# Gates kept raw until the merge, a scan-ordered S5 state, and S5 begun inside the attention, in a hybrid decoder block

## The chip, the cores and the metric

The kernel runs on one core of a Trainium2 chip. The metric is the device time of the program in microseconds (us): 1381.73 us is the median of three runs of the kernel before (1381.71 to 1381.80). The engines are named as the profile names them: PE is TensorE's matmul, PEld its weight load, DVE is VectorE, ACT is ScalarE, POOL is GpSimd, SP is SyncE, whose queue issues the DMAs here.

## The reference

One decoder block over 1024 tokens of width 1024, in float32. Two branches share one normed input: sliding-window attention (8 query heads, 2 key/value heads, blocks of 128 tokens, window 128, learned sinks and a bias by distance) and an S5 state space model (512 channels in 32 groups of 16, 64 complex states each). Sigmoid gates merge them, and a squared-ReLU MLP follows.

```
h = rmsnorm(x);  q, k, v, u, gate_a, gate_s = split(h @ w_in)
attn  = attention(q, k, v, sinks, bias) @ w_attn_branch
s     = gelu(s5_scan(u) + d_skip * u)          # tanh form
s     = s * sigmoid(s @ w_glu)
mixed = sigmoid(gate_a) * attn + sigmoid(gate_s) * (s @ w_ssm_branch)
y     = x + rmsnorm(mixed @ w_out);   out = y + rmsnorm(relu(h2 @ w1)^2 @ w2)
```

## The kernel before

Every float32 product is three products of rounded halves: a value is split into hi (ACT copies it rounded, L154 for weights, L161 for activations) and lo (the remainder, by DVE in L156 and L162), and mm3 (L172 to L174) adds hi·hi, hi·lo and lo·hi into one PSUM bank of 512 columns. The kernel has eight banks. Program order is the order on each engine: nothing is reordered, so an instruction that waits holds up everything written after it for the same engine. All loads and stores go through SP's queue, weights included, which arrive in pieces of 128x1024 (raw) and are split by L154 and L156 one piece ahead of their use.

The stages in order, and what the change touches in them:

- **qkv** projects the queries, the S5 input u, the keys and the values. u_evac stores u to DRAM (ud) with the token index split as k·8+j, so that a row of S5 input holds the 128 chunks k of eight tokens. L366 makes the lo parts of the keys on DVE. v_evac (L371) transposes the values on PE.
- **attention** has 16 halves (a block of 128 tokens and one key/value head) in 20 software-pipelined steps. A step puts on PE the scores of half i (L521, L522), the product with the values of half i-3 (L568) and the transposes of half i-2 (L554), then one or two pieces of filler: twelve projection matmuls each, for the gates (L1036) and, from the last steps, for stage 1. DVE adds the bias and takes the maximum (L525), ACT does Exp (L538), POOL divides (L544), ACT and DVE split the transposed probabilities. In each step from i=2, `tick(8)` feeds a side generator: ssm_tables, which computes the powers of the S5 state matrix and the tables of S5 on DVE in many small instructions (L42 in the trace, where all recorded operations have one line), runs four groups of small matmuls on PE (kernel_part, L807), adds the skip weight (L815) and stores the tables to DRAM (qd and kd). Whatever is left of them is drained behind the last step.
- **stage 1** multiplies the attention's output with its branch weights: per output tile 24 projection matmuls for the gate, a Sigmoid (L973), 12 matmuls of the branch, a product on DVE (L986) and a store (md). After each 12 matmuls `tick(11)` feeds the **ssm** generator: load1 reads u and the input weights (L850, L853), inputs() makes 8 groups of small matmuls (L869) that ACT copies into the state F, load2(0) reads the tables of the first half of the channels (L857, L861), scan() runs 18 complex multiply-adds (macc, L880 to L884, five DVE instructions) over the 128 chunks, stack() swaps halves, and outputs() runs 16 small matmul pairs per bank (L917, L918) and the tanh GELU (L921 to L927), then stores z to DRAM (zd). outputs(1) and its tables load2(1) come behind outputs(0).
- **gates 6 and 7 and glu**: z is read back (L997), split, multiplied with the glu weights (mm3), its sigmoid taken (L1019, L1020), and split again into zz. **stage 2** reads the gates (sd) and the attention branch (md) back, multiplies zz with its branch weights, multiplies by the gate (L1068), adds (L1069, POOL) and splits. The output projection and the MLP follow and are untouched.

A sequential index over 1024 tokens is split in three levels for the scan: eight tokens i in a chunk, and 128 chunks k = a·8+b. macc walks b inside each a, then carries over a.

Of the kernel before, what the change touches and what calls it, by code (L numbers as in the profile page):

```python
# [8 lines left out]
F32 = mybir.dt.float32  # L9
# [3 lines left out]
AF = mybir.ActivationFunctionType  # L13
# [4 lines left out]
P = 128  # L18
# [88 lines left out]
class Block:  # L107
# [276 lines left out]
    def u_evac(self, ps, g, h):  # L384

        nc = self.nc
        if g % 2 == 0 and h == 0:
            self.ut[g // 2] = self.r([2, 8, P])
        ut = self.ut[g // 2][:, g % 2]
        nc.scalar.activation(out=ut[:, :, 64 * h:64 * h + 64], in_=ps.rearrange("p (k j) -> p j k", j=8), func=AF.Copy)  # L390
        if h:
            nc.sync.dma_start(out=self.ud[g * P:g * P + P], in_=ut)

    def qkv(self):
        nc = self.nc
# [28 lines left out]
        for qt in range(4):  # L424
            h = qt // 2
# [47 lines left out]
        sc = self.r([2, G, 256])  # L473
        self.PT = [self.q([2, 512], F32R) for _ in range(2)]
        self.scores = [sc[:, 0], sc[:, 1], self.q([G, 256])]
        piece = self.wq.get()
        for h in range(2):
            ps = self.proj(piece, h)
            if h:
                self.wq.done()  # L480
                self.wq.pump()
            self.k_evac(ps, h)
        piece = self.wq.get()
        vt = []
        for h in range(2):
            vt.append(self.t([512]))
            ps = self.proj(piece, h)
            if h:
                self.wq.done()
                self.wq.pump()  # L490
            self.nc.scalar.activation(out=vt[h], in_=ps, func=AF.Copy)
# [84 lines left out]
    def attention(self, filler):  # L576

        late = {}

        def go(key):  # L580
            if key in late:
                next(late[key], None)

        halves = [(n, kv) for n in range(8) for kv in range(2)]
        st = {}
        for i in range(len(halves) + 4):
            if i < 16:
                n, kv = halves[i]
                if kv == 0:
                    st[n] = {"mx": self.small(NH, "mx")}  # L590
                self.a_scores(n, kv, st[n])
            go("old sm")
            if 3 <= i < 19:
                n, kv = halves[i - 3]
                late["pv"] = self.a_pv(n, kv, st[n])
                next(late["pv"])
            if 2 <= i < 18:
                n, kv = halves[i - 2]
                self.a_trans(n, kv, st[n])
            go("old pv")  # L600
            go("pv")
            late["old pv"] = late.pop("pv", iter(()))
            if i < 16:
                n, kv = halves[i]
                late["sm"] = self.a_softmax(n, kv, st[n])
                next(late["sm"])
            late["old sm"] = late.pop("sm", iter(()))
            for _ in range(1 + (4 <= i < 17) if i < 19 else 0):
                next(filler, None)
            if i >= 2:  # L610
                self.tick(8)
            if i == 0:
                self.v_evac(self.v_late, 1)

# [225 lines left out]
    def ssm(self):  # L840


        nc = self.nc
# [9 lines left out]
                nc.sync.dma_start(out=xT[hf][(7 - j) * 16:(8 - j) * 16], in_=udv[j])  # L853

        def load2(hf):
            T[hf], Q[hf] = self.r([16, P]), self.r([16, P])
            nc.sync.dma_start(out=Q[hf], in_=self.qd[hf].rearrange("c s q a t -> (c s) (q a) t"))  # L857
            kd = self.kd[256 * hf:256 * hf + 256]
            for r in range(8):
                src = bass.AP(kd.tensor, kd.offset + 16 * r, [[240, 16], [16 * 240, 16], [1, P]])  # L860
                nc.sync.dma_start(out=T[hf][r * 16:(r + 1) * 16], in_=src)  # L861

        def inputs(hf):
            for ri in range(2):
                for qb in range(2):
                    ps = self.ps().rearrange("p (q k) -> p q k", q=4)
                    for q in range(4):
                        for a in range(2):
                            nc.tensor.matmul(ps[a * DH:a * DH + DH, q, :], lhsT=W1[hf][:, ri, qb * 4 + q, a * DH:a * DH + DH],  # L869
                                             rhs=xT[hf][:, 2 * (qb * 4 + q) + a, :], start=True, stop=True)  # L870
                    q0 = 8 * hf + 4 * qb
                    nc.scalar.activation(out=F[:, ri, q0:q0 + 4, 1:P], in_=ps[:, :, 0:P - 1], func=AF.Copy)
                    yield "wait"

        def macc(dst, src, i, n):
# [8 lines left out]
            v.tensor_tensor(out=dst, in0=dst, in1=t1, op=ALU.add)  # L884

        def scan():
            Fv = F.rearrange("p c q (a b) -> p c q a b", b=8)
            for b in range(1, 8):
                macc(Fv[:, :, :, :, b], Fv[:, :, :, :, b - 1], 0, 16)
                yield 14  # L890
            for j, i in ((1, 7), (2, 8), (4, 9), (8, 10)):
                macc(Fv[:, :, :, j:16, 7], Fv[:, :, :, 0:16 - j, 7], i, 16 - j)
                yield 14
            for b in range(7):
                macc(Fv[:, :, :, 1:16, b], Fv[:, :, :, 0:15, 7], b, 15)
                yield 14

        def stack(hf):
# [9 lines left out]
        def outputs(hf):  # L908
            for gb in range(4):

                if gb % 2 == 0:
                    zt = self.q([8, P])
                ps = self.ps()
                for gi in range(4):
                    gg = gb // 2 * 8 + gb % 2 + 2 * gi
                    o = ps[:, gi * P:(gi + 1) * P]
                    nc.tensor.matmul(o, lhsT=T[hf][:, gg, :], rhs=xT[hf][:, gg, :], start=True, stop=False)  # L917
                    nc.tensor.matmul(o, lhsT=Q[hf][:, gg, :], rhs=F[:, gg % 2, 8 * hf + gg // 2, :], start=False, stop=True)  # L918

                y2, w = self.t([512]), self.t([512])  # L920
                nc.scalar.activation(out=y2, in_=ps, func=AF.Square)  # L921
                v.tensor_scalar(out=y2, in0=y2, scalar1=0.044715, scalar2=1.0, op0=ALU.mult, op1=ALU.add)
                v.tensor_tensor(out=w, in0=y2, in1=ps, op=ALU.mult)
                yield "wait"
                nc.scalar.activation(out=w, in_=w, func=AF.Tanh, scale=GELU_C)
                g4 = lambda a: a.rearrange("p (g k) -> p g k", g=4)
                v.scalar_tensor_tensor(out=zt[:, gb % 2:8:2, :], in0=g4(w), scalar=1.0, in1=g4(ps), op0=ALU.add, op1=ALU.mult)  # L927
                yield "wait"
                if gb % 2:
                    r0 = 256 * hf + gb // 2 * P  # L930
                    zv = self.zd[r0:r0 + P].rearrange("(g d) i k -> i d g k", d=16)
                    for i in range(8):
                        nc.sync.dma_start(out=zv[i], in_=zt[i * 16:(i + 1) * 16])
# [9 lines left out]
            yield from inputs(hf)  # L943
        tmp = self.q([2, 512])
        load2(0)
        yield from scan()
        yield from stack(0)
        yield from stack(1)
        yield "wait"
        yield from outputs(0)  # L950
        load2(1)
        for _ in range(5):
            yield "wait"
        yield from outputs(1)


    def stage1(self):
# [32 lines left out]
    def glu(self):  # L990
# [14 lines left out]
        for mp in range(2):  # L1005
            wh, wl = self.wq.get()
            for mi in range(2):
                m = mp * 2 + mi
                cs = slice(mi * P, mi * P + P)
                for h in range(2):  # L1010
                    ks = slice(64 * h, 64 * h + 64)
                    part = lambda z: z.rearrange("p (i k) -> p i k", i=8)[:, :, ks]
                    ps = self.ps()
                    self.mm3(ps, [((wh[:, k, cs], wl[:, k, cs]), (part(zh[k // 2][:, k % 2]), part(zl[k // 2][:, k % 2]))) for k in range(4)])
                    if (mi, h) == (1, 1):
                        self.wq.done()
                        self.wq.pump()
                    sg = self.t([8, 64])
                    nc.scalar.activation(out=sg, in_=ps.rearrange("p (i k) -> p i k", i=8), func=AF.Sigmoid, scale=0.5)  # L1019
                    nc.vector.scalar_tensor_tensor(out=sg, in0=part(zf[mp][:, mi]), scalar=0.5, in1=sg, op0=ALU.mult, op1=ALU.mult)  # L1020
                    hi, lo = (self.zz[h][:, c, m].rearrange("p (k i) -> p i k", i=8) for c in range(2))
                    self.split(sg, hi, lo)


    def gates(self, ds):
        nc = self.nc
        for d in ds:
            piece = self.wq.get()
            for h in range(2):
# [3 lines left out]
                    self.wq.done()  # L1033
                    self.wq.pump()
                sg = self.t([512])
                nc.scalar.activation(out=sg, in_=ps, func=AF.Sigmoid)  # L1036
                nc.sync.dma_start(out=self.sd[d * P:(d + 1) * P, 512 * h:512 * h + 512], in_=sg)


    def stage2(self):  # L1040
# [13 lines left out]
        for h in range(2):  # L1054
            hi, lo = self.big([8, 512]), self.big([8, 512])
            self.mT.append((hi, lo))
            sig, zz = sigs[h], self.zz[h]
            mas = ma[h]
            for dp in range(4):
                sb = self.wq.get()  # L1060
# [243 lines left out]
    def run(self):  # L1304
        with self.tc.manual_schedule():
# [1 line left out]
            self.qkv()  # L1307
            self.sd = self.dram.tile([D, L], F32, name="sd")
            s1 = self.stage1()
            self.side = [self.ssm_tables()]  # L1310
            self.attention(itertools.chain(self.gates(range(6)), s1))
            self.drain()
            self.side = [self.ssm()]
            for _ in s1:
                self.tick(11)
            self.drain()
            glu = self.glu()
            next(glu)
# [87 lines left out]
```

## Time and profile before

| | us |
|---|---|
| median of three runs | 1381.73 |
| the profiled execution's own time | 1382.77 |
| its span, first to last instruction | 1380.6 |
| mean granted clock of TensorE | 0.974 |
| PE busy | 1300.3 (94%) |
| DVE busy | 775.5 (56%) |
| ACT busy | 470.7 (34%) |
| POOL busy | 120.7 (9%) |

The span divides at the following times: queries, u, keys and values until 135.2, attention and the drained tables until 304.2, stage 1 with S5's inputs and scan until 436.4, S5's outputs and the first gate matmuls until 477.3, gates 6 and 7 until 499.1, glu until 525.7, stage 2 until 573. What comes after, 807 us, is the output projection and the MLP.

How to read it: PE is busy 94% of the span, but its busy time has a clock in it. The granted clock is a share of full speed, and the same 512 columns take 0.23 us or 0.42 us from start to start by the level of that clock. So a stretch is read three ways: how long it lasts, how much of it PE had work, and at which clock.

### The profile page before, as it was taken

To read this page: it belongs to the slowest core of one execution; us is meant where nothing else is said; L and a number is where in the kernel's file an instruction comes from. 1 tells how busy PE (TensorE), PEld (TensorE's weight loads), DVE (VectorE), ACT (ScalarE), POOL (GpSimd) and SP (SyncE) were. 2 spreads that over 40 slices of the span, in tenths; PEclk is the share of its full clock that TensorE was granted. 3 is DMA by queue.
4 is the path that set the end of the run, shared out by engine and by line. 5 is a ranking of instruction groups with operands and counts; after the bars stand their busy time and mean duration, and the time that the engine had idled before them with its cause. 6 is when DMAs were issued, how large, how long until landed. Compare 5 with 4: busy or idle time off the path is not lost.

```text
span 1380.6 us, 15685 instructions
## 1 busy us (share of the span) xinstructions
PE 1300.3 (94%) x6144; PEld 1074.8 (78%) x6144; DVE 775.5 (56%) x1367; ACT 470.7 (34%) x797; POOL 120.7 (9%) x79
## 2 busy tenths in 40 slices
PE   8999998879988499998999999999999999999997
PEld 7988876657767487876878888888888888888886
DVE  5773766661799246647862544455444554445556
ACT  4434787742112144345543112211122111221132
POOL 1000212100000003333300000000000000000014
PEclk9999999989989699999999999999999999999999
DMA  8313111248622658445611112111111111111142
GB/s 335 136 64 107 47 38 63 72 108 178 115 69 74 93 154 319 153 155 186 238 47 42 50 31 62 46 47 60 32 61 47 46 51 42 61 47 46 40 182 98
DMA packets 55065, 132.61 MB, mean 96 GB/s; under 512 B 5072, under 2 KB 22224, under 8 KB 53712
## 3 DMA queue, kind: packets, MB, share of 16 engines
q1 hardware_dynamic: 54992, 131.62, 31.2%
q8 instruction: 48, 0.79, 0.2%
q14 instruction: 25, 0.20, 0.0%
HBM read 105.94 MB, written 25.66 MB: 95 GB/s over the span
## 4 chain that ended last, share of the span: by engine, by line
PE 59%; DVE 4%; ACT 2%; DMA 1%; issue 1%; SPq 0%; DVEq 0%; ACTq 0%
PE ps L173 18%; PE ps L174 18%; PE ps L172 18%; PE ps L1152 1%; PE ps L1153 1%; PE ps L1151 1%; DVE lo L156 1%; DMA r<-kd 1%; ACT t L247 1%; DVE r L1090 1%; DMA r<-qd 0%; DVE b L162 0%; ACT b L161 0%; ACT r L1108 0%; PE ps L917 0%
## 5 line engine op out<-in xcount | busy, mean ns | idle before, releaser
L172 PE MATMUL ps<-b,hi 128*128 128x512 f32 x976 | 387.3, 397 | 7.7 <-DVE t L815 5.4
L174 PE MATMUL ps<-b,lo 128*128 128x512 f32 x976 | 383.6, 393 | 7.8 <-DVE lo L156 7.8
L173 PE MATMUL ps<-b,hi 128*128 128x512 f32 x976 | 383.3, 393 | 0.9 <-DVE b L162 0.9
L154 ACT ACTIVATE hi<-raw 128x1024 fp32r<-128x1024 f32 x124 | 129.0, 1051 | 284.2 <-issue 242.3
L172 PEld LDWEIGHTS ps<-b,hi 128*128 128x128 f32 x976 | 185.3, 190 | 49.5 <-DVE t L815 5.6
L174 PEld LDWEIGHTS ps<-b,lo 128*128 128x128 f32 x976 | 185.1, 190 | 48.1 <-DVE lo L156 8.9
L173 PEld LDWEIGHTS ps<-b,hi 128*128 128x128 f32 x976 | 185.5, 190 | 39.3 <-DVE b L162 1.5
L156 DVE TENSOR_TENSOR lo<-raw,hi 128x1024 fp32r<-128x1024 f32 x122 | 154.1, 1275 | 105.4 <-ACT hi L154 104.8
L1245 DVE TENSOR_TENSOR b<-b,ps 128x512 f32<-128x512 f32 x208 | 139.3, 685 | 99.0 <-PE ps L174 99.0
L174 PE MATMUL ps<-hi,r 128*128 128x512 f32 (+1 forms) x482 | 187.1, 388 | 0.0
L173 PE MATMUL ps<-lo,r 128*128 128x512 f32 (+1 forms) x482 | 187.1, 388 | 0.0
L172 PE MATMUL ps<-hi,r 128*128 128x512 f32 (+1 forms) x482 | 187.1, 388 | 0.0
L1186 DVE TENSOR_TENSOR t<-t 128x512 f32<-128x512 f32 x64 | 44.2, 691 | 164.1 <-ACT t L1185 164.1
L172 PEld LDWEIGHTS ps<-hi,r 128*128 128x128 f32 x482 | 90.5, 188 | 18.7
L173 PEld LDWEIGHTS ps<-lo,r 128*128 128x128 f32 x482 | 90.5, 188 | 18.7
L174 PEld LDWEIGHTS ps<-hi,r 128*128 128x128 f32 x482 | 90.5, 188 | 18.6
L1185 ACT ACTIVATE t<-ps 128x512 f32<-128x512 f32 x64 | 38.2, 597 | 190.1 <-PE ps L174 190.1
L1299 POOL TENSOR_TENSOR t<-b,r 128x512 f32<-128x512 f32 (+1 forms) x17 | 20.5, 1227 | 663.8 <-DVE b L1296 663.8
L162 DVE TENSOR_TENSOR r<-t,r 128x512 fp32r<-128x512 f32 x64 | 44.3, 692 | 44.9 <-ACT r L161 44.9
L161 ACT ACTIVATE r<-t 128x512 fp32r<-128x512 f32 x64 | 40.5, 633 | 49.9 <-DVE t L1186 49.0
L1152 PE MATMUL ps<-lo,b 128*128 128x512 f32 x128 | 51.5, 403 | 3.9 <-DVE lo L156 3.7
L1151 PE MATMUL ps<-hi,b 128*128 128x512 f32 x128 | 51.4, 402 | 1.7 <-DVE b L162 1.0
(199 smaller groups left out, 1487.9 us busy)
## 6 DMA issues: line engine op xcount, KB each, us to landing
raw<-in_ff_dram SPq DMA_DIRECT2D x64, 512.0 KB, 3.8
raw<-in_win_dram SPq DMA_DIRECT2D x26, 512.0 KB, 4.6
raw<-in_wout_dram SPq DMA_DIRECT2D x24, 512.0 KB, 4.1
r<-in_x_dram SPq DMA_DIRECT2D x14, 512.0 KB, 6.2
sd<-t SPq DMA_DIRECT2D x16, 256.0 KB, 2.1
md<-t SPq DMA_DIRECT2D x16, 256.0 KB, 2.4
raw<-in_wsb_dram SPq DMA_DIRECT2D x8, 512.0 KB, 7.7
b<-sd SPq DMA_DIRECT2D x2, 2048.0 KB, 13.8
```

Source lines behind the costliest of these rows:

```text
L154: nc.scalar.activation(out=hi, in_=src, func=AF.Copy)
L156: return (hi, lo), lambda: eng.tensor_tensor(out=lo, in0=src, in1=hi.bitcast(F32), op=ALU.subtract)
L161: nc.scalar.activation(out=hi, in_=src, func=AF.Copy)
L162: (eng or nc.vector).tensor_tensor(out=lo, in0=src, in1=hi.bitcast(F32), op=ALU.subtract)
L172: self.nc.tensor.matmul(ps, lhsT=ah, rhs=bh, start=first and i == 0, stop=False)
L173: self.nc.tensor.matmul(ps, lhsT=ah, rhs=bl, start=False, stop=False)
L174: self.nc.tensor.matmul(ps, lhsT=al, rhs=bh, start=False, stop=last and i == n - 1)
L1151: nc.tensor.matmul(ac[c], lhsT=a, rhs=wh[:, cs], start=k == 0, stop=False)
L1152: nc.tensor.matmul(ac[c], lhsT=a, rhs=wl[:, cs], start=False, stop=False)
L1185: nc.scalar.activation(out=rl, in_=ps, func=AF.Relu)
L1186: nc.vector.tensor_tensor(out=rl, in0=rl, in1=rl, op=ALU.mult)
L1245: nc.vector.tensor_tensor(out=a, in0=a, in1=ps, op=ALU.add)
```

## The change

Four things are done, in the functions above.

1. **Gates raw.** gates() evacuates its PSUM bank with Copy in place of Sigmoid. stage2 takes the Sigmoid of the reloaded gate tiles, four ACT instructions on 128x2048 elements. In all, the program has 5 ACT_TABLE_LOADs where it had 29.
2. **Chunks in scan order.** u is stored with chunk k = a·8+b at position b·16+a, so the scan's operands are runs of 16 neighbouring elements where they were 16 elements eight apart. The shift by one chunk between input and state becomes two copies per bank in inputs() (eight ACT instructions more). glu's matmuls now read 64 runs of 8 elements where they read 8 runs of 64, and the split into zz writes with an inner step of 64 elements where it was 8.
3. **Earlier.** ssm_tables starts with the keys' projection (`proj_ticks(11)`), ticks come in every step, and at i=15 what is left of the tables is drained and ssm begins. Stage 1 ticks 9 in place of 11.
4. **Both sets of tables at once.** load2(0) and load2(1) are issued one behind the other ahead of the scan (the second Q in two tiles of the pool that ssm_tables used), then both stacks, then outputs(0) and outputs(1) with nothing between.

```diff
@@ u_evac
-        nc.scalar.activation(out=ut[:, :, 64 * h:64 * h + 64], in_=ps.rearrange("p (k j) -> p j k", j=8), func=AF.Copy)
+        ut4 = ut.rearrange("p j (b a) -> p j b a", b=8)
+        nc.scalar.activation(out=ut4[:, :, :, 8 * h:8 * h + 8], in_=ps.rearrange("p (a b j) -> p j b a", b=8, j=8), func=AF.Copy)
@@ qkv
+        self.side = [self.ssm_tables()]
         piece = self.wq.get()
-        for h in range(2):
-            ps = self.proj(piece, h)
+        for h, ps in self.proj_ticks(piece, 11):
...
-        for h in range(2):
+        for h, ps in self.proj_ticks(piece, 11):
             vt.append(self.t([512]))
-            ps = self.proj(piece, h)
@@ attention
-            if i >= 2:
-                self.tick(8)
+            if i == 15:
+                self.drain()
+                self.side = [self.ssm()]
+            self.tick(8)
@@ ssm
         def load2(hf):
-            T[hf], Q[hf] = self.r([16, P]), self.r([16, P])
-            nc.sync.dma_start(out=Q[hf], in_=self.qd[hf].rearrange("c s q a t -> (c s) (q a) t"))
+            T[hf] = self.r([16, P])
+            if hf:
+                Q[hf] = [self.qp.tile([P, 8, P], F32, tag="qp", name="qp") for _ in range(2)]
+            else:
+                both = self.r([16, P])
+                Q[hf] = both[:, 0:8], both[:, 8:16]
+            qd = self.qd[hf].rearrange("c s q a t -> (c s) (q a) t")
+            for i in range(2):
+                nc.sync.dma_start(out=Q[hf][i], in_=qd[:, 8 * i:8 * i + 8])
...
-                    nc.scalar.activation(out=F[:, ri, q0:q0 + 4, 1:P], in_=ps[:, :, 0:P - 1], func=AF.Copy)
+                    nc.scalar.activation(out=F[:, ri, q0:q0 + 4, 16:P], in_=ps[:, :, 0:P - 16], func=AF.Copy)
+                    nc.scalar.activation(out=F[:, ri, q0:q0 + 4, 1:16], in_=ps[:, :, P - 16:P - 1], func=AF.Copy)
...
-            Fv = F.rearrange("p c q (a b) -> p c q a b", b=8)
+            Fv = F.rearrange("p c q (b a) -> p c q b a", b=8)
             for b in range(1, 8):
-                macc(Fv[:, :, :, :, b], Fv[:, :, :, :, b - 1], 0, 16)
+                macc(Fv[:, :, :, b], Fv[:, :, :, b - 1], 0, 16)
...
         load2(0)
+        load2(1)
         yield from scan()
-        yield from stack(0)
-        yield from stack(1)
-        yield "wait"
-        yield from outputs(0)
-        load2(1)
-        for _ in range(5):
-            yield "wait"
-        yield from outputs(1)
+        for hf in range(2):
+            yield from stack(hf)
+        for hf in range(2):
+            yield from outputs(hf)
@@ glu
-                    part = lambda z: z.rearrange("p (i k) -> p i k", i=8)[:, :, ks]
+                    part = lambda z: z.rearrange("p (m a) -> p m a", a=16)[:, :, 8 * h:8 * h + 8]
...
-                    hi, lo = (self.zz[h][:, c, m].rearrange("p (k i) -> p i k", i=8) for c in range(2))
-                    self.split(sg, hi, lo)
+                    hi, lo = (self.zz[h][:, c, m].rearrange("p (a b i) -> p i b a", b=8, i=8) for c in range(2))
+                    self.split(sg.rearrange("p (i b) a -> p i b a", i=8), hi, lo)
@@ gates
-                nc.scalar.activation(out=sg, in_=ps, func=AF.Sigmoid)
+                nc.scalar.activation(out=sg, in_=ps, func=AF.Copy)
@@ stage2
+            for b in range(2):
+                nc.scalar.activation(out=sig[:, 4 * b:4 * b + 4], in_=sig[:, 4 * b:4 * b + 4], func=AF.Sigmoid)
@@ run
-            self.side = [self.ssm_tables()]
             self.attention(itertools.chain(self.gates(range(6)), s1))
-            self.drain()
-            self.side = [self.ssm()]
             for _ in s1:
-                self.tick(11)
+                self.tick(9)
```

How the instructions stand, at three places. First DVE at the end of the keys' and values' projections, before; r_1135 is the keys' lo part, r_1272 the values':

```order
L506 TENSOR_SCALAR nsink<-gn 128x8
L156 TENSOR_TENSOR lo<-raw,hi 128x1024
L366 TENSOR_TENSOR r_1135<-ps,r_1134 64x512 x8
L156 TENSOR_TENSOR lo<-raw,hi 128x1024
L162 TENSOR_TENSOR r_1272<-ps,r_1272 128x8x64
L525 ISA r_1136,mx<-ps,r_1130 128x128
```

The same place after, from the second half of the keys on (b_472 and qp hold the tables, dg a diagonal):

```order
L366 TENSOR_TENSOR r_1135<-ps,r_1134 64x512 x4
L156 TENSOR_TENSOR lo<-raw,hi 128x1024
L42 COPY b_472<-b_472 64x16x16 x2
L42 TENSOR_REDUCE dg<-ident 128x16
L42 TENSOR_TENSOR qp<-b_472 128x576
L42 TENSOR_TENSOR b_472<-b_472 128x576
L42 TENSOR_TENSOR qp<-qp,b_472 128x576
```

The last three rows stand twice (real and imaginary part), 22 small table instructions stand ahead of each group of four L366, and PE now has the first eight kernel_part matmuls right behind the values' projection, ahead of v_evac's transposes.

Then ACT in one step of the attention, before; r_1136 are scores, b_767 the attention's output:

```order
L538 ACT_TABLE_LOAD
L538 ACTIVATE r_1136,rs<-r_1136,nm 128x256 x4
L540 ACTIVATE es<-es 128x4
L1036 ACT_TABLE_LOAD
L1036 ACTIVATE t_1820<-ps 128x512
L161 ACTIVATE r_1137<-ps 128x512
L161 ACTIVATE r_1138<-ps 128x512
L161 ACTIVATE b_767<-t_1806 64x512
L571 ACTIVATE t_1898<-ps 64x512
```

and after, where the gate's Copy is line 1042:

```order
L538 ACTIVATE r_1136,rs<-r_1136,nm 128x256 x4
L540 ACTIVATE es<-es 128x4
L1042 ACTIVATE t_2053<-ps 128x512
L161 ACTIVATE r_1137<-ps 128x512
L161 ACTIVATE r_1138<-ps 128x512
L161 ACTIVATE b_767<-t_2039 64x512
L571 ACTIVATE t_2133<-ps 64x512
```

Both table loads of the step are gone. Last SP's queue around the tables of S5's second half, before:

```order
L933 DMA zd<-r_3591 16x8x128 x8
L933 DMA zd<-r_3637 16x8x128 x8
L857 DMA r_3679<-qd 128x2048
L861 DMA r_3678<-kd 16x16x128 x8
L933 DMA zd<-r_3689 16x8x128 x8
L933 DMA zd<-r_3730 16x8x128 x8
L997 DMA b_3771<-zd 128x2x1024 x2
```

and after:

```order
L994 DMA md<-t_2938 128x512
L866 DMA r_3004<-qd 128x1024 x2
L870 DMA r_3003<-kd 16x16x128 x8
L866 DMA qp<-qd 128x1024 x2
L870 DMA r_3015<-kd 16x16x128 x8
L66 DMA raw<-in_wab_dram 128x1024
L994 DMA md<-t_3033 128x512
```

The loads from qd and kd for the second half moved from between the two halves' z stores to directly behind those of the first half, early in stage 1.

## Rows read from the trace of the kernel before

**Rows 1.** Stretches: us; busy PE, PEld, DVE, ACT, POOL; PEclk; DMA share; GB/s
```profile
135.20:304.20 169.00, 145.13 (x766) 114.85 (x764) 112.72 (x342) 119.20 (x258) 29.31 (x20) 0.96 0.20 57
304.20:351.60 47.40, 47.40 (x288) 36.88 (x285) 8.61 (x11) 9.19 (x14) 0.15 (x1) 0.96 0.75 164
351.60:436.40 84.80, 76.98 (x327) 62.78 (x326) 82.30 (x112) 12.86 (x17) 0.00 (x0) 0.94 0.37 87
436.40:477.30 40.90, 16.33 (x130) 16.17 (x128) 13.38 (x25) 8.03 (x14) 0.00 (x0) 0.71 0.57 103
```

**Rows 2.** PE's waits: line, awaited engine and line; us in total, times, longest
```profile
PE ps L917 <- DMA r<-kd: 24.6, 1, 24.6
PE ps L807 <- DVE qp L42: 8.1, 4, 2.9
PE ps L174 <- DVE lo L156: 7.8, 2, 6.4
```

**Rows 3.** PE's timeline, an undisturbed step: start us, us, engine, line, operation, tiles
```profile
161.34 0.28 PE L521 MATMUL ps<-r,b 128*128 128x256 f32 x1
...
164.01 0.48 PE L172 MATMUL ps<-b,hi 128*128 128x512 f32 x1
...
169.57 0.28 PE L521 MATMUL ps<-r,b 128*128 128x256 f32 x1
```

**Rows 4.** PE's timeline, first inputs group, and the first outputs half's two ends
```profile
322.76 1.09 PE L869 MATMUL ps<-r,r 128*64 128x128 f32 x16
...
436.39 0.38 PE L917 MATMUL ps<-r,r 128*128 128x128 f32 x2
...
443.31 0.39 PE L918 MATMUL ps<-b,r 128*128 128x128 f32 x2
```

**Rows 5.** Groups on ACT, 135 to 530 us: busy us, mean ns; idle before, releaser
```profile
L154 ACT ACTIVATE hi<-raw 128x1024 fp32r<-128x1024 f32 x23 | 24.2, 1053 | 11.2 <-PE ps L173 7.3 <-issue 3.9
L538 ACT ACT_TABLE_LOAD x13 | 16.7, 1283 | 30.7 <-DVE nm L535 28.9 <-issue 1.8
L1036 ACT ACT_TABLE_LOAD x12 | 15.4, 1283 | 0.2
```

**Rows 6.** PE's timeline behind the four table waits: first and tenth matmul
```profile
304.19 0.80 PE L172 MATMUL ps<-b,hi 128*128 128x512 f32 x1
...
308.20 0.46 PE L172 MATMUL ps<-b,hi 128*128 128x512 f32 x1
```

**Rows 7.** Groups on DVE, 135 to 530 us, by shape: scan and weight split
```profile
L880 DVE TENSOR_TENSOR r<-b,GW 128x512 f32<-128x512 f32 x7 | 7.9, 1132 | 1.1 <-ACT b L872 1.0
L881 DVE TENSOR_TENSOR r<-b,GW 128x256 f32<-128x256 f32 x7 | 4.4, 631 | 0.0
L883 DVE TENSOR_TENSOR r<-r 128x512 f32<-128x512 f32 x7 | 4.8, 693 | 0.2
L883 DVE TENSOR_TENSOR r<-r 128x256 f32<-128x256 f32 x1 | 0.4, 424 | 0.0
L884 DVE TENSOR_TENSOR b<-b,r 128x512 f32<-128x512 f32 x7 | 8.2, 1170 | 0.2
L156 DVE TENSOR_TENSOR lo<-raw,hi 128x1024 fp32r<-128x1024 f32 x23 | 28.1, 1222 | 46.9 <-ACT hi L154 46.7
```

**Rows 8.** DVE's timeline: the keys' lo parts, one small and one larger table instruction
```profile
119.72 1.38 DVE L366 TENSOR_TENSOR r<-ps,r 64x512 fp32r<-64x512 f32 x2 [1.32 <-ACT r L364]
...
186.42 0.17 DVE L42 TENSOR_TENSOR GW<-GW 128x16 f32<-128x16 f32 x1
...
298.76 0.76 DVE L42 TENSOR_TENSOR qp<-b 128x576 f32<-128x576 f32 x1
```

**Rows 9.** SP's DMA queue: S5's input for one half of the channels
```profile
316.04 9.13 SPq L853 DMA_DIRECT2D r<-ud  x8
```

**Rows 10.** DVE's timeline: the GELU's last operation in two successive output banks
```profile
479.68 0.69 DVE L927 SCALAR_TENSOR_TENSOR r<-t,ps 128x512 f32<-128x512 f32 x1 [0.70 <-DMA zd<-r]
...
482.20 0.69 DVE L927 SCALAR_TENSOR_TENSOR r<-t,ps 128x512 f32<-128x512 f32 x1 [0.70 <-ACT t L925]
```

More of the change, by code (lines that the diff above doesn't have):

```diff
@@ L886, in scan @@
         def scan():
-            Fv = F.rearrange("p c q (a b) -> p c q a b", b=8)
+            Fv = F.rearrange("p c q (b a) -> p c q b a", b=8)
             for b in range(1, 8):
-                macc(Fv[:, :, :, :, b], Fv[:, :, :, :, b - 1], 0, 16)
+                macc(Fv[:, :, :, b], Fv[:, :, :, b - 1], 0, 16)
                 yield 14
             for j, i in ((1, 7), (2, 8), (4, 9), (8, 10)):
-                macc(Fv[:, :, :, j:16, 7], Fv[:, :, :, 0:16 - j, 7], i, 16 - j)
+                macc(Fv[:, :, :, 7, j:16], Fv[:, :, :, 7, 0:16 - j], i, 16 - j)
                 yield 14
             for b in range(7):
-                macc(Fv[:, :, :, 1:16, b], Fv[:, :, :, 0:15, 7], b, 15)
+                macc(Fv[:, :, :, b, 1:16], Fv[:, :, :, 7, 0:15], b, 15)
                 yield 14
@@ L917, in outputs @@
                     nc.tensor.matmul(o, lhsT=T[hf][:, gg, :], rhs=xT[hf][:, gg, :], start=True, stop=False)
-                    nc.tensor.matmul(o, lhsT=Q[hf][:, gg, :], rhs=F[:, gg % 2, 8 * hf + gg // 2, :], start=False, stop=True)
+                    nc.tensor.matmul(o, lhsT=Q[hf][gg // 8][:, gg % 8, :], rhs=F[:, gg % 2, 8 * hf + gg // 2, :], start=False, stop=True)
                 y2, w = self.t([512]), self.t([512])
@@ L1010, in glu @@
                 for h in range(2):
-                    ks = slice(64 * h, 64 * h + 64)
-                    part = lambda z: z.rearrange("p (i k) -> p i k", i=8)[:, :, ks]
+                    part = lambda z: z.rearrange("p (m a) -> p m a", a=16)[:, :, 8 * h:8 * h + 8]
                     ps = self.ps()
@@ L1017, in glu @@
                         self.wq.pump()
-                    sg = self.t([8, 64])
-                    nc.scalar.activation(out=sg, in_=ps.rearrange("p (i k) -> p i k", i=8), func=AF.Sigmoid, scale=0.5)
+                    sg = self.t([64, 8])
+                    nc.scalar.activation(out=sg, in_=ps.rearrange("p (m a) -> p m a", a=8), func=AF.Sigmoid, scale=0.5)
                     nc.vector.scalar_tensor_tensor(out=sg, in0=part(zf[mp][:, mi]), scalar=0.5, in1=sg, op0=ALU.mult, op1=ALU.mult)
-                    hi, lo = (self.zz[h][:, c, m].rearrange("p (k i) -> p i k", i=8) for c in range(2))
-                    self.split(sg, hi, lo)
+                    hi, lo = (self.zz[h][:, c, m].rearrange("p (a b i) -> p i b a", b=8, i=8) for c in range(2))
+                    self.split(sg.rearrange("p (i b) a -> p i b a", i=8), hi, lo)
     def gates(self, ds):
```

## The prediction

> **What bounds the kernel now.** PE is busy 94% of the span, so I looked for the stretches in which it isn't, or in which it is busy at a low clock, and asked of each how much work it holds. Three views do this: the table by stretches, where busy PE and PEclk stand beside the length [rows 1], PE's waits with what they ended on [rows 2], and PE's timeline for the price of undisturbed work [rows 3]. The profiled execution took 1382.77 us with a span of 1380.6, 1.04 above the median of 1381.73. All sums are made against 1382.77, and the 1.04 is taken off at the end.
>
> The price of work comes from one quiet step of the attention [rows 3]. From 161.34 to 164.01 PE does 8 scores, 4 products with the values and 8 transposes (2.67 us), from 164.01 to 169.57 it does 24 projection matmuls (5.56 us, so 2.78 for a piece of twelve). With these prices I counted each stretch [rows 1]:
>
> - Attention and tables last 169.0. Work: 32 pieces of filler (89.0), 14 full halves at 2.67 (37.4), the two halves of the first block at half that (2.7), the four table groups at about 1.2 each (4.8, estimated from the like group of small matmuls at 1.09 [rows 4]), the values' transposes 0.6: 134.5. **Excess 34.5.**
> - Stage 1 lasts 47.4 + 84.8 = 132.2. Work: 40 pieces (111.2) and 8 input groups at 1.09 (8.7): 119.9. **Excess 12.3**, with 7.8 of it the waits for lo [rows 2], the rest the clock.
> - The outputs' stretch lasts 40.9. Work: two halves of 7.1 [rows 4], 14.2. **Excess 26.7**, with 24.6 of it the one wait for the load from kd [rows 2], the rest the clock that follows the idle time (0.71 in this stretch).
>
> Together 73.5 us of excess, on 1382.77.
>
> **Part by part: what is removed.**
>
> *Table loads.* In the attention Exp and Sigmoid take turns on ACT: 13 loads at L538, 12 at L1036, 1283 ns each [rows 5]. A load at L538 stands between DVE's maximum and Exp, the one at L1036 delays the copies and splits queued behind it, the transposed probabilities among them, on which the next product with the values waits. A pair of steps has four loads, 5.1 us of ACT; the 34.5 are spread over some eight such steps and the drained tables. The order shows that a step has no load left. The Sigmoid returns in stage 2 as four instructions of 128x2048. L154 takes 1.053 us for 1024 elements of a row [rows 5], so some 2 us each, 8 in all. Only DVE's product with the gate needs them, and eight PSUM banks let PE run ahead of it: I cost them at 0, and at 4 (one instruction for each half) if PE runs out of banks.
>
> *Tables drained behind the attention.* [...] In the new order the tables are done inside the attention, as ticks start some seven steps earlier. This gain is in the 34.5.
>
> *The second half's tables.* The 24.6 are a transfer issued behind outputs(0) for outputs(1). Now it is issued before the scan, some 80 us ahead of its use. Nothing else is late there: T and Q were the only operands loaded. I count all 26.7.
>
> *The scan.* DVE is busy 82.3 of 84.8 us in the scan's stretch [rows 1], so the lo splits behind it come late, and PE waits. A macc was 1.132 + 2·0.631 + 0.693 + 1.170 = 4.26 us; L883 alone, which reads and writes neighbouring elements, takes 0.693 for the 512 elements that cost L880 and L884 1.13 and 1.17 [rows 7]. So with runs of 16 I take 3·0.693 + 2·0.424 = 2.93. Per output tile of stage 1 (36 matmuls, 8.3 us) the ticks bring 27/14 = 1.93 macc, 5.65 us, and DVE also has L986 (0.7, as L883) and three quarters of an L156 (0.92): 7.3, below 8.3. Before it was 33/14 = 2.36 macc, 10.0, and 1.6 beside it: 11.6, above. The 12.3 go.
>
> **What is added or takes their place.**
>
> *A stall at the values.* PE's queue now has the first table group right behind the values' projection, which ends at 135.2, where the first stretch begins [rows 1]. What DVE does before it can be added up: the keys' first lo parts start at 119.72 [rows 8], the second half's one half projection later, near 126, and end near 130. Ahead of each of the two groups stand 22 small instructions at no more than 0.17 [rows 8], 2.4 to 3.7 a group; part of the first group falls into idle time. So the second lo parts end near 132.5, then L156 (1.22), two copies and a reduction (1), six instructions of 576 elements (4.4 at 0.73): 139.0. PE stands from 135.2 to 139.0: 3.8, 0.5 until the first matmul's end, 1.5 for the clock: **5.8** (bounds 2 and 8). Behind it on PE are v_evac and the first scores, so the whole attention shifts.
>
> *Waits that come to light.* In the attention each removed delay leaves the next one: POOL's division for the first halves, DVE's lo parts of the probabilities, the last steps, where there is little filler and Exp, division, transposes and product follow one another. I take **5.5**, bounds 0 and 9 (a quarter of the 34.5).
>
> *S5 begun early.* The input of one half takes 9.1 us to load [rows 9], both 18.3; from step 15 to the first input group PE has some 21 us of work by the prices above (about six pieces of filler, the last products and transposes). 0.5, up to 9.1 if the loads wait for tiles. Eight more copies on ACT are off the path.
>
> *Outputs in one go.* DVE and ACT need 2.5 us for the GELU of a bank (479.68 to 482.20 [rows 10]), PE 1.8 (a quarter of 7.1). Before, the halves were apart; now eight banks follow, the delay of 0.7 a bank adds up over all of them, and the last z leaves some 2 us later behind PE's last output than it did. Gates 6 and 7 are eight pieces, 22 us, which must cover the GELU's end, z's way through DRAM and its splits; I assume that they covered these just so: 2 us, bounds 0 and 5. Lo waits and outputs themselves 0.5 each.
>
> Sum: 5.8 + 5.5 + 0.5 + 2 + 1 = 14.8. Then 1382.77 - 73.5 + 14.8 = 1324.1, less 1.04: **1323**. With the bounds of the added terms (4 to 32, not all at once), the forecast's own range is 1314 to 1332.
>
> **glu's short runs.** glu now reads its moving operand in 64 runs of 8 elements. No row shows such a matmul; the nearest are matmuls on contiguous columns at 0.23 each (5.56 for 24 [rows 3]), and DVE's instructions on single elements eight apart, 1.6 to 1.7 times slower than on neighbouring ones (1132 and 1170 against 693 [rows 7]). I take 0, since a run of 8 is nearer to contiguous than single elements are; the upper bound is a rival below. The same for the split into zz: its writes have an inner step in both versions, and lie on ACT and DVE, which glu leaves time.
>
> [...]
>
> **The rivals.**
>
> - *The scan stays slow* (0.12). If the broadcast operand sets L880's time, and not the stride, macc stays 4.26: 1.93 of them, 8.2, and 1.6 beside make 9.8 against 8.3 per tile, 1.5 late in each of ten tiles, less 5 of slack, plus 1 of clock: +11, **1334**. For it: L881 takes 631 for 256 elements, L883 only 424, and both operands differ. Against it: L884 has no broadcast and is as slow as L880.
> - *glu at half rate* (0.10). 96 matmuls lose 0.23 each, +22: **1345**.
> - *S5's tiles wait* (0.09). The inputs need the tiles that scores, bias and keys leave with the last steps; SP holds the weights queued behind. One load late, 9, and the clock: **1333**.
> - *ACT was not the limit* (0.06). If DVE or POOL set the pace of the attention's steps, half of the 34.5 stays: +15, **1338**. Against it: DVE is busy 112.7 and POOL 29.3 of 169 [rows 1].
> - *Slower* (0.04). One mechanism does it: short runs cost PE a fixed time each. The gain of 59 is gone at 0.61 us more per glu matmul, 0.84 in place of 0.23, or 13 ns for each run of 8; beyond 13 ns the kernel is slower, at 15 ns (0.96) 96·0.73 = 70 more, **1393**. Nothing in the trace shows such a price.
>
> **How the numbers follow.** The forecast has 0.59. Its own range, with the scan, S5's tiles and ACT's rival, fills 1312 to 1342 with 8 in 10; glu at half rate lies outside. What a measurement can tell from no change is 0.2%, 2.8 us. All but the slower rival are faster by more: faster 0.95, same 0.01, slower 0.04.
>
> **What would show it.** In the profile after: two table loads in the attention's stretch; steps of 8.2 to 8.6 us; a wait of the table group behind the values of about 4 us; L880 on 512 elements near 0.7 us; DVE under 90% in stage 1 and no wait for lo above 1 us; no wait of PE for a load from kd; glu's matmuls still 0.23 apart. The prediction is wrong if a step stays at 10 or more, if macc stays above 4, or if glu takes 45 us in place of 25.

## The result, and the profile after

The changed kernel takes 1323.76 us (median of four runs, 1321.83 to 1325.34) against 1381.76: a ratio of 0.9578 [0.9562, 0.9595], 58.0 us less. 1323 was forecast. The total is right; two of the terms behind it are not, and they cancel, so that it fits to 1 us is luck.

The profiled execution took 1321.83 us, 1.9 less than the median, its span is 1320.0; the readings below are of this execution. The table by stretches, columns as in [rows 1], cut at the values' projection, the first wait for S5's input, the outputs, gates 6 and 7, and glu:

```profile
135.20:140.45 5.25, 1.58 (x17) 0.78 (x16) 4.10 (x6) 1.54 (x2) 0.00 (x0) 0.74 0.61 150
140.45:280.50 140.05, 138.80 (x763) 116.52 (x760) 106.04 (x292) 86.49 (x232) 29.11 (x20) 0.99 0.32 83
280.50:399.20 118.70, 114.83 (x585) 93.14 (x585) 69.86 (x125) 20.97 (x37) 0.00 (x0) 0.99 0.61 130
399.20:416.20 17.00, 17.00 (x142) 16.48 (x141) 10.05 (x17) 8.45 (x14) 0.00 (x0) 1.00 0.42 87
416.20:438.10 21.90, 21.90 (x99) 17.90 (x97) 10.08 (x14) 8.18 (x13) 0.00 (x0) 1.00 0.83 198
438.10:465.30 27.20, 25.51 (x107) 20.11 (x106) 17.05 (x19) 16.54 (x21) 0.00 (x0) 1.00 0.48 161
```

From the end of the values' projection to gate 6 it was 342.1 us (135.2 to 477.3 [rows 1]) and is 281.0. The work priced for it in the prediction is 134.5 + 119.9 + 14.2 = 268.6. So 73.5 us over the work became 12.4. The rest hardly moved: glu and the first wait of stage 2 took 26.6 and take 27.2, and what follows took 854.9 (1380.6 less 525.7) and takes 854.7 (1320.0 less 465.3).

PE's waits and, from its timeline, the places where the 12.4 lie (the last wait, of 0.9, is glu's and not part of them; beside the waits, the matmul records show the clock: 0.63 or 0.80 us long where it was granted at 0.50, from 286.19 to 287.65):

```profile
PE ps L878 <- DMA r<-ud: 3.9, 1, 3.9
PE ps L809 <- DVE qp L42: 3.7, 2, 2.0
PE ps L172 <- ACT t L1042: 1.3, 2, 1.0
PE ps L173 <- DVE r L162: 0.9, 1, 0.9
```

```profile
134.99 0.39 PE L174 MATMUL ps<-b,lo 128*128 128x512 f32 x1
137.38 0.38 PE L809 MATMUL ps<-qp,b 128*32 128x128 f32 x2 [2.01 <-DVE qp L42]
139.42 1.10 PE L809 MATMUL ps<-qp,b 128*32 128x128 f32 x14 [1.66 <-DVE qp L42]
140.45 1.12 PE L374 MATMUL ps<-ident,t 128*128 128x128 f32 x4
...
280.13 0.39 PE L174 MATMUL ps<-b,lo 128*128 128x512 f32 x1
284.38 1.88 PE L878 MATMUL ps<-r,r 128*64 128x128 f32 x16 [3.87 <-DMA r<-ud]
286.19 0.80 PE L172 MATMUL ps<-b,hi 128*128 128x512 f32 x1
286.78 0.63 PE L173 MATMUL ps<-b,hi 128*128 128x512 f32 x1
...
289.92 1.09 PE L878 MATMUL ps<-r,r 128*64 128x128 f32 x16
```

Behind the values PE stands until 140.45: 5.25 us with 1.2 of table work in it, 4.05. At S5's first inputs it stands 3.87, and the group with its twelve matmuls then takes 5.54 (284.38 to 289.92) where the next takes 3.96 (289.92 to 293.88): 5.4 together. That leaves 2.9 for all of the attention. About 1.8 of it is the clock after the first stall, granted at 0.50 from 139.42 to 144.40: from the values' transposes at 140.45 to the fifth step at 159.41 it took 19.0, and the same work before (135.22 to 153.56) took 18.3 with a wait of 1.15 for POOL in it.

The groups of the scan and the table loads, as in [rows 5, 7]:

```profile
L538 ACT ACT_TABLE_LOAD x1 | 1.3, 1283 | 1.8 <-DVE nm L535 1.8
L980 ACT ACT_TABLE_LOAD x1 | 1.3, 1283 | 0.0
L890 DVE TENSOR_TENSOR r<-b,GW 128x512 f32<-128x512 f32 x7 | 4.8, 686 | 5.0 <-ACT b L882 5.0
L891 DVE TENSOR_TENSOR r<-b,GW 128x256 f32<-128x256 f32 x7 | 2.9, 418 | 0.0
L893 DVE TENSOR_TENSOR r<-r 128x512 f32<-128x512 f32 x7 | 4.8, 693 | 0.2
L894 DVE TENSOR_TENSOR b<-b,r 128x512 f32<-128x512 f32 x7 | 4.8, 692 | 0.2
L173 PE MATMUL ps<-r,hi 128*128 128x512 f32 x32 | 12.8, 399 | 0.9 <-DVE r L162 0.9
```

The last row in the kernel before:

```profile
L173 PE MATMUL ps<-r,hi 128*128 128x512 f32 x32 | 12.6, 393 | 0.0
```

A macc takes 0.686 + 2·0.418 + 0.693 + 0.692 = 2.91 us, against 2.93 forecast. glu's matmuls on runs of 8 take 399 ns each; before it was 393 in the same 32 of the program. The rival of half rate is out.

### The profile page after: what moved, and what is told of

It reads as the page before. It is cut to its first block, busy times and chain, and to the rows that moved or that the text cites. A ratio compares the mean times of both kernels' runs of the same rounds, so it can differ in the third digit from the quotient of the medians.

```text
span 1320.0 us, 15673 instructions
## 1 busy us (share of the span) xinstructions
PE 1285.9 (97%) x6144; PEld 1069.8 (81%) x6144; DVE 757.7 (57%) x1367; ACT 446.8 (34%) x785; POOL 120.3 (9%) x79
## 4 chain that ended last, share of the span: by engine, by line
PE 72%; DVE 13%; ACT 7%; DMA 4%; issue 3%; SPq 1%; POOL 1%; DVEq 0%; ACTq 0%
PE ps L172 21%; PE ps L173 21%; PE ps L174 21%; DVE lo L156 2%; ACT r L538 2%; DVE b L162 2%; DVE r L162 1%; ACT hi L154 1%; PE ps L1160 1%; PE ps L1161 1%; PE ps L1159 1%; DVE r L525 1%; DMA raw<-in_wsb_dram 1%; DMA r<-ud 1%; DMA raw<-in_win_dram 1%
## 5 line engine op out<-in xcount | busy, mean ns | idle before, releaser
L172 PE MATMUL ps<-b,hi 128*128 128x512 f32 x976 | 384.0, 393 | 1.7 <-ACT t L1042 1.3
L154 ACT ACTIVATE hi<-raw 128x1024 fp32r<-128x1024 f32 x124 | 128.9, 1051 | 276.8 <-issue 239.4
L172 PEld LDWEIGHTS ps<-b,hi 128*128 128x128 f32 x976 | 183.8, 188 | 41.5 <-ACT t L1042 1.7
L156 DVE TENSOR_TENSOR lo<-raw,hi 128x1024 fp32r<-128x1024 f32 x122 | 155.2, 1284 | 105.5 <-ACT hi L154 105.3
L1253 DVE TENSOR_TENSOR b<-b,ps 128x512 f32<-128x512 f32 x208 | 139.4, 685 | 99.0 <-PE ps L174 99.0
L172 PE MATMUL ps<-hi,r 128*128 128x512 f32 (+1 forms) x482 | 187.1, 388 | 0.0
L172 PEld LDWEIGHTS ps<-hi,r 128*128 128x128 f32 x482 | 90.5, 188 | 18.7
L173 PEld LDWEIGHTS ps<-lo,r 128*128 128x128 f32 x482 | 90.5, 188 | 18.7
L161 ACT ACTIVATE r<-t 128x512 fp32r<-128x512 f32 x64 | 40.5, 633 | 49.9 <-DVE t L1194 49.0
```

The costliest lines, as they stand in the source:

```text
L154: nc.scalar.activation(out=hi, in_=src, func=AF.Copy)
L156: return (hi, lo), lambda: eng.tensor_tensor(out=lo, in0=src, in1=hi.bitcast(F32), op=ALU.subtract)
L161: nc.scalar.activation(out=hi, in_=src, func=AF.Copy)
L172: self.nc.tensor.matmul(ps, lhsT=ah, rhs=bh, start=first and i == 0, stop=False)
L173: self.nc.tensor.matmul(ps, lhsT=ah, rhs=bl, start=False, stop=False)
L1253: nc.vector.tensor_tensor(out=a, in0=a, in1=ps, op=ALU.add)
```

## Experiments: each part alone, and each part undone

The names b1 to b4 are the kernel before with one part of the change, a1 to a4 the changed kernel with one part taken back. The kernel before had a median of 1382.4 beside both sets; the column of a is against 1323.76, measured beside 1381.76, so its numbers may be too high by some 0.7.

| part | alone on the kernel before | taken out of the changed kernel |
|---|---|---|
| gates raw (no table loads) | 1365.59: -16.8 | 1342.47: +18.7 |
| chunks in scan order | 1369.54: -12.8 | 1329.85: +6.1 |
| both sets of tables at once | 1360.84: -21.5 | 1347.52: +23.8 |
| tables and S5 begun early | 1378.13: -4.2, ratio 0.9969 [0.9958, 0.9981] | 1336.13: +12.4 |
| sum | -55.3 | +61.0 |

The whole change is -58.0, between the two sums, so the parts nearly add up; where the columns differ, parts lean on one another.

**Table loads.**

```diff
 # a1: the changed kernel, gates()
+                nc.scalar.activation(out=sg[:, 0:1], in_=ps[:, 0:1], func=AF.Sigmoid)
                 nc.scalar.activation(out=sg, in_=ps, func=AF.Copy)
 # b1: the kernel before, gates() and stage2()
-                nc.scalar.activation(out=sg, in_=ps, func=AF.Sigmoid)
+                nc.scalar.activation(out=sg, in_=ps, func=AF.Copy)
...
+            for b in range(2):
+                nc.scalar.activation(out=sig[:, 4 * b:4 * b + 4], in_=sig[:, 4 * b:4 * b + 4], func=AF.Sigmoid)
```

> The changed kernel, with one Sigmoid of a single column ahead of each gate's Copy, so that ACT loads its tables as often as in the kernel before and nothing else comes back. If the loads set the pace of the attention's steps: steps of 9.1 to 9.9 us in place of 8.2 while gates are made, +20 to +25, 1344 to 1349. If another engine set the pace: +6 at most, under 1330.

> The kernel before with the gates kept raw alone (Copy in the attention, Sigmoid at the merge). If the table loads set the pace of the steps: steps of 8.2 us, -20 to -25, 1357 to 1362, and the drained tables still cost 12. If not: -6 at most.

Measured: +18.7 and -16.8, both a little short of what was expected and far from the rival. a1's ACT groups have the 13 and 12 loads again, and PE's waits show how they are paid:

```profile
PE ps L172 <- DVE mx L525: 9.5, 3, 6.1
PE ps L172 <- DVE t L817: 5.6, 1, 5.6
```

These two lines are a1's; the changed kernel has no such wait. L525 and L817 are DVE instructions that free a PSUM bank. Steps did not become 9.1 to 9.9 us long all over: in a1 three successive steps take 8.24 (their first scores start at 181.25, 189.50 and 197.74, the next at 205.97), two later ones as well, others 8.6 to 16.7. I expected an even slowing; it comes in lumps, as if PE ran ahead until no bank was free. a1's longest wait, on ACT, DVE and PE:

```profile
271.66 1.28 ACT L538 ACT_TABLE_LOAD   x1 [1.30 <-DVE nm L535]
275.03 1.04 ACT L154 ACTIVATE hi<-raw 128x1024 fp32r<-128x1024 f32 x1
276.11 1.23 DVE L156 TENSOR_TENSOR lo<-raw,hi 128x1024 fp32r<-128x1024 f32 x1 [4.32 <-ACT hi L154]
278.20 0.79 PE L172 MATMUL ps<-b,hi 128*128 128x512 f32 x1 [6.09 <-DVE mx L525]
```

On ACT a weight split (L154) stands behind the load and Exp; DVE stands in L156 until it is done, and L525, next on DVE, frees the bank only behind that. The other two long waits, 3.02 at 174.04 and 5.60 at 234.62 (L817), come in the same way, behind an L156 that stood 3.05 and 4.32 us for L154. The pair of runs shows the cause, the loads (the one-column Sigmoids themselves are 0.17 us each on ACT). A part of what a1 loses comes back later: at S5's inputs it waits 1.7 us where the changed kernel waits 3.9.

**Scan order.**

```diff
 # a2: the changed kernel (b2: the reverse, on the kernel before); u, inputs and glu likewise
-            Fv = F.rearrange("p c q (b a) -> p c q b a", b=8)
+            Fv = F.rearrange("p c q (a b) -> p c q a b", b=8)
             for b in range(1, 8):
-                macc(Fv[:, :, :, b], Fv[:, :, :, b - 1], 0, 16)
+                macc(Fv[:, :, :, :, b], Fv[:, :, :, :, b - 1], 0, 16)
```

> The changed kernel with the old order of chunks: u, inputs, scan and glu as before, all else as changed. If the stride costs the scan: L890 at 512 elements back at 1.13 us, DVE short by 1.5 us per output tile in stage 1, +11 (0 to 15), 1335. If the fewer ticks (9 for 11) and the earlier start leave enough room: +2, 1326.

> The kernel before with the chunks in scan order alone. macc 2.93 in place of 4.26 us; at 2.36 macc per output tile DVE then has 6.9 and 1.6, as much as the 8.3 of PE: -12, 1370, the waits for lo gone. If those waits come from elsewhere: no change beyond 2.

b2 came as expected, and no wait for lo is left in its stage 1. a2 lost 6.1, between the two cases: the waits for lo are back, shorter than the 7.8 of [rows 2]:

```profile
PE ps L174 <- DVE lo L156: 3.4, 2, 2.2
L888 DVE TENSOR_TENSOR r<-b,GW 128x512 f32<-128x512 f32 x7 | 7.9, 1131 | 5.0 <-ACT b L880 4.9
```

So something else in the change had already taken half of that wait. The fewer ticks (9 for 11) are the likely part, since b4, which starts early but keeps 11 ticks, still waits 9.2 us for lo; no run changes the ticks alone in the old order. By this the two edits pay for the same 12.

**Both sets of tables.**

```diff
 # b3: the kernel before, ssm() (a3: the reverse, on the changed kernel)
         load2(0)
+        load2(1)
         yield from scan()
-        yield from stack(0)
-        yield from stack(1)
-        yield "wait"
-        yield from outputs(0)
-        load2(1)
-        for _ in range(5):
-            yield "wait"
-        yield from outputs(1)
+        for hf in range(2):
+            yield from stack(hf)
+        for hf in range(2):
+            yield from outputs(hf)
```

> The changed kernel with the second half's tables loaded behind outputs(0) again. If the transfer cannot be hidden there: one wait of PE for kd of 20 us or more, +26, 1350. If the earlier scan leaves enough work behind outputs(0): +10, 1334.

> The kernel before with both sets of tables loaded ahead of the scan and the outputs back to back, alone. The wait of 24.6 goes and the clock with it: -26, 1355. If the transfer is late there too, or the eight banks of GELU in one go hold up glu: -15 to -20.

a3 has the wait back at 23.8 us and is 23.8 slower. b3 gained 21.5 of 26: its 24.6 are gone, and in their place stand waits that were not there, from PE's timeline:

```profile
435.09 0.46 PE L925 MATMUL ps<-b,r 128*128 128x128 f32 x2 [0.93 <-DVE b L912]
475.35 0.50 PE L172 MATMUL ps<-r,hi 128*128 128x512 f32 x1 [1.41 <-ACT r L161]
476.80 0.50 PE L173 MATMUL ps<-r,hi 128*128 128x512 f32 x1 [0.95 <-DVE r L162]
```

The outputs wait for the stack, and glu for z's splits. I read this as the forecast's term for glu, 2 us: with the halves back to back, z is as late as eight banks of GELU make it. No run alters the GELU alone.

**Early start.**

```diff
 # a4: the changed kernel (b4: the reverse, on the kernel before); K and V without ticks likewise
-            if i == 15:
-                self.drain()
-                self.side = [self.ssm()]
-            self.tick(8)
+            if i >= 2:
+                self.tick(8)
```

> The changed kernel with the tables and S5 begun where they were begun before (first tick at i=2, drain and ssm behind the attention). Drained tables cost 12.6 again; the stall behind the values (4.0 and 1.5 of clock) and the wait for u (3.9 and about 2 of clock) go: +1, 1325. If the early start is worth what the drain cost: +12, 1336.

> The kernel before with the tables begun at the keys and S5 at i=15, alone. The drained tables' 12.6 go, the stall behind the values (5.5) and the wait for u (6) come: -1, 1381. If the early start is worth what the drain cost: -12, 1370.

This expectation failed: taken out of the changed kernel the early start costs 12.4, not 1. PE's waits in a4:

```profile
PE ps L808 <- DVE qp L42: 8.1, 4, 2.9
PE ps L927 <- DVE b L914: 4.6, 1, 4.6
PE ps L555 <- POOL r L545: 2.6, 4, 1.2
```

The drained tables cost their 8.1 again, as expected. What I had left out is the second row: with 9 ticks and a late start the scan does not end in time, and the outputs wait 4.6 us for the stack (L914). The third row is a wait of the attention that the changed kernel lacks. With these two rows the expected +1 becomes some 8; the rest of the 12.4 was not apportioned. In the kernel before (b4) the same start is worth 4.2. Its waits show where the drained tables' 8.1 went:

```profile
PE ps L918 <- DMA r<-kd: 21.7, 1, 21.7
PE ps L172 <- ACT t L1037: 8.7, 2, 5.9
```

L1037 is the gate's Sigmoid, for which the kernel before has 12 table loads of 1283 ns [rows 5]: with the tables moved into the attention's steps, PE waits 8.7 us for it, where the kernel before waits 2.9 for L1036, the same line. So in b4 a good part of what the drain gives back seems to be lost again in the steps that the loads hold up. In the changed kernel the early start seems to be two things: it takes the tables out of the end of the attention, which the rows show, and it lets 9 ticks do, which they suggest; no run has the late start with 11 ticks, or the tables early and S5 late.

## Experiments: the two stalls that are left

c1 puts the first table group one tick later, c2 S5's first input group two ticks later, c3 does both, c4 does both with 10 ticks in stage 1.

```diff
 # c1, c3, c4: ssm_tables
             yield from play(4)
             yield "wait"
+            if q4 == 0:
+                yield "wait"
             ps = kernel_part(q4, Q)
 # c2, c3, c4: ssm
-        for _ in range(4):
+        for _ in range(6):
             yield "wait"
         for hf in range(2):
             yield from inputs(hf)
 # c4: run
-                self.tick(9)
+                self.tick(10)
```

> The changed kernel with one tick more ahead of the first group of table matmuls, which then stands behind a piece of filler and not right behind the values' projection. The wait of 3.7 us and its clock go: -5, 1318.5. If DVE is as late at the new place, or the later groups are pushed into the drain: 0 to -2.

> The changed kernel with S5's first input group two ticks (two pieces of filler) later. The wait of 3.9 us for u and about 2 of clock go: -5.5, 1318. If the scan, two pieces later, makes the outputs late: 0 to -2.

> Both of these edits. If the two stalls are separate: -10, 1313.

> The kernel with both edits (first table group one tick later, inputs two ticks later) and 10 in place of 9 per tick in stage 1. In it glu's first matmuls waited 2.5 and 1.0 us for z's splits and ran about 2 us longer at the lower clock. If z is late because the scan is emitted late: the scan needs 252 of credit, 28 ticks at 9 and 25 at 10, outputs start two to three pieces of filler earlier, those waits go, -4, 1315. If DVE (2.14 macc at 2.93 and 1.6 beside per 8.3 us, 95%) then makes the lo splits late: 0 or +2.

| | us | against 1323.76 |
|---|---|---|
| c1, table group later | 1323.66 | -0.1 |
| c2, inputs later | 1322.88 | -0.9 |
| c3, both | 1318.75 | -5.0 |
| c4, both and 10 ticks | 1315.52 | -8.2 |

The kernel before had a median of 1382.51 beside c1 to c3 and 1381.82 beside c4. c1 and c2 removed their waits and gained no more than the changed kernel's own runs spread (1321.83 to 1325.34); the timelines tell where it went. First c1's, then c2's:

```profile
148.41 0.81 PE L554 MATMUL ps<-ident,r 128*128 128x128 f32 x4 [2.55 <-POOL r L544]
284.70 1.97 PE L880 MATMUL ps<-r,r 128*64 128x128 f32 x16 [5.82 <-DMA r<-ud]
```

```profile
435.67 0.50 PE L172 MATMUL ps<-r,hi 128*128 128x512 f32 x1 [1.98 <-ACT r L161]
437.12 0.79 PE L173 MATMUL ps<-r,hi 128*128 128x512 f32 x1 [0.95 <-DVE r L162]
438.14 0.63 PE L172 MATMUL ps<-r,hi 128*128 128x512 f32 x1
```

In c1, PE no longer stands behind the values, so it comes to the third step sooner, where POOL's first division is not done (2.55), and to S5's inputs sooner, whose last load lands at the same time as before (284.70 and 284.38), since on SP the loads stand behind the tables' last stores and start at 269.3 where they started at 268.2: there it waits 5.82 in place of 3.87. In c2 the inputs come without a wait, but the scan and z then come late, and glu waits 1.98 more and runs its first matmuls more slowly: the twelve from 437.71 to 442.83 have records of 0.63 us, those from 443.14 on of 0.39 to 0.40.

In c1 the stall removed ahead of a wait for a transfer moved in part to that wait, and in c2 the wait came out again behind the scan, in glu. c3, with both edits, gains more than c1 and c2 together. c4 lets the scan come out earlier again, and glu's first wait goes (1.98 in c2, 2.46 in c3); the one of 0.95 stays. c4 is the fastest here, 0.9525 [0.9512, 0.9538] of the kernel before. Between c3 and c4 stand 3.2 us where 4 were expected, or 2.5 with the difference of 0.7 between the two medians of the kernel before.

## Why the prediction held, point by point

- **The price of work and the excess**: right. The stretch that held 73.5 us over the priced work now holds 12.4; 14.8 were forecast, 2 of them for glu, which lies outside this stretch.
- **Table loads**: right in mechanism. The forecast put 34.5 on the attention as a whole and did not part it. b1 shows that the loads are 16.8 of it; the drained tables' waits are another 8.1, which b1 and a4 still have, and behind them the clock was granted at 0.50 in the kernel before, from 304.19 to 308.20: nine matmuls took 4.01 us there [rows 6], where nine later ones took 2.09 (308.50 to 310.59). b4's 4.2 and a4's 12.4 are not the price of the drain, since these edits move S5 as well. The four Sigmoids in stage 2 were put at 0, and from stage 2 on the time is the same (854.7 for 854.9).
- **The second half's tables**: right, 23.8 (a3) and 21.5 (b3), with 26.7 counted.
- **The scan**: the price of a macc was right to 0.02 us, and b2's 12.8 is the 12.3 that were counted. The rival of a broadcast operand is out: L890 fell from 1132 to 686 ns with the same broadcast.
- **The stall at the values**: 5.8 forecast. DVE's last table instruction was put at 139.0, it ended at 139.4; PE lost 4.05 and about 1.8 by the clock. No run shows the 1.5 that the forecast held for the clock, which was my estimate; the 1.8 is what stood in its place.
- **Waits that come to light in the attention**: forecast 5.5, measured 1.1 beside that clock, which is L1042's wait (1.3) within the rounding of the prices. This term was too large by 4.4. POOL's division, which I named, waits in c1 (2.9), b1 and a4 (2.6 each), but not in the changed kernel: the stall behind the values gives POOL the time.
- **S5 begun early**: forecast 0.5, measured 5.4. This term was too small by 4.9, and two steps of it failed: the time that a set of loads takes, and the time that PE needs to come to them. SP's queue in the changed kernel, and DVE's product that the store ahead of the loads waits for:

```profile
257.55 2.61 SPq L836 DMA_DIRECT2D qd<-qp  x4
267.25 0.33 SPq L994 DMA_DIRECT2D md<-t  x1
267.76 0.33 SPq L819 DMA_DIRECT2D kd<-t  x1
268.18 0.41 SPq L852 DMA_DIRECT2D r<-w1d  x1
268.68 5.84 SPq L855 DMA_DIRECT2D r<-ud  x8
275.43 0.34 SPq L852 DMA_DIRECT2D r<-w1d  x1
276.65 11.32 SPq L855 DMA_DIRECT2D r<-ud  x8
```

```profile
266.53 0.69 DVE L993 TENSOR_TENSOR t<-t,ps 128x512 f32<-128x512 f32 x1 [4.02 <-ACT t L980]
```

 The 9.13 of [rows 9] is the time in which SP issued the second set, not the time from the first issue to the last landing. Here the eight issues of the first set began at 268.68, and PE was let go by the last of them at 284.38: 15.7 us for a set, where I took 9.1. The profile's part on DMA issues gives a median of 10.2 us from issue to landing in this stretch. In the kernel before the same set was issued from 306.96 and used at 322.76 without a wait that showed, so 15.8 was there as an upper bound.

 The other step is the 21 us of work on PE. PE was ready for the inputs at 280.5 (284.38 less 3.87), only 12.3 us after the first load was issued at 268.18. SP had been free since 260.2, but stage 1's first store (md) and the tables' last (kd) stand ahead of the loads in its queue, and md's product came late on DVE, behind ACT's Sigmoid (L980). With 21 us ahead a set of 15.7 would have been in time, and with 12.3 a set of 9.1 as well: it took both errors to make the wait.
- **glu**: forecast 2, measured 0.6 (27.2 for 26.6). Within it three things changed: glu's first matmuls wait 0.9 for z's split, its 96 matmuls at 6 ns more make 0.6, and a wait of 1.1 for ACT at the start of stage 2 (L172 <- L161 at 524.50 before) is gone.
- **Lo waits and outputs**: forecast 0.5 each. Neither shows: stage 1 has no wait for lo (L156), and the outputs' stretch of 17.0 is the priced 14.2 and one piece of 2.8.

The two wrong terms are -4.4 and +4.9. Either alone would have moved the forecast by 4 to 5 us, inside its range. That the sum fits to 1 us has a second piece of luck in it: the terms come to 13.0 where 14.8 were forecast, so the profiled execution was 1321.83 where 1324.1 was forecast, but it lies 1.9 below its median, and the one before lay 1.04 above.

## What to carry to other kernels

Price one undisturbed step, count the work of every stretch by it, and the excess says what there is to win, whatever line the waits name. When a stall is taken away, look at once for the next fixed point on the engine's path, above all a transfer with its own start: in c1 what was won ahead of it was lost there, since the transfer did not start earlier. For a set of loads, take the time from the first issue to the first use that needs the last of them, and look at what stands ahead of them in their queue and what that waits for.

## What the runs showed of the hardware

- The stride that an instruction of DVE reads and writes with decided its time at equal size: 512 float32 elements in runs of 16 took 0.686 to 0.693 us, and 1.132 to 1.170 with elements 32 bytes apart, with or without a broadcast operand. On TensorE the moving operand in runs of 32 bytes took 399 ns a matmul in place of 393.
- In the changed kernel two waits of PE cost over four tenths of their length again in clock. After the 3.87 us at S5's inputs the next group with its twelve matmuls took 1.6 us longer, its matmuls 0.63 us in place of 0.39 at first, at a granted clock of 0.53 from 284.30 to 287.65. After the 4.05 us behind the values it was 0.50 from 139.42 to 144.40, and cost about 1.8 us.
- ACT's table loads took 1283 ns in the mean in the kernel before (29 loads), the changed kernel (5) and a1 (26 from 130 to 470 us); 24 of them more, with 16 one-column Sigmoids, made this kernel 18.7 us slower (a1), 0.78 us for each load.
